# Additions to x on the gate tiles' ring, memsets on GpSimd, a shorter compressed softmax, an early Exp table and another bank for the first latent values

## The chip, the core and the metric

One core of a Trainium2 chip runs the whole kernel: TensorE (PE), VectorE (DVE), ScalarE (ACT), GpSimd (POOL) and the DMA queue of SyncE (SP). The metric is the device time in microseconds; the kernel before took 1947.82, the median of three runs (1947.81 to 1949.94).

## What is computed

Two layers of a transformer on 512 positions of width 1024, in float32. Each layer is half a SwiGLU, a mixer, half a SwiGLU, each on a normed x; the first layer's mixer is "even" (compressed, selected and sliding attention with gates, beside dilated attention), the second's is MLA (latent) attention. Cut to what matters:

```python
for l in range(DEPTH):
    x = x + 0.5 * _swiglu(_rms_norm(x, ffn1_norm[l]), ...)
    h = _rms_norm(x, mix_norm[l])
    x = x + (_even_mixer(h, ...) if l % 2 == 0 else _mla_mixer(h, ...))
    x = x + 0.5 * _swiglu(_rms_norm(x, ffn2_norm[l]), ...)
return _rms_norm(x, final_norm)
```

The compressed attention's part that the change touches: keys and values are compressed to 31 blocks of 32 positions (16 apart), and query t sees a block only if the block has ended, so the first 31 queries see none and get zero:

```python
s = jnp.where(mask, scores, -MASK_BIG)
p = jnp.where(mask, jnp.exp(s - max(s)), 0.0)
p_c = p / where(sum(p) > 0, sum(p), 1.0)
out = gate0 * (p_c @ vc) + gate1 * o_selected + gate2 * o_window
```

## The kernel before

x lies transposed, as eight tiles x[0] to x[7] of 128 features by 512 positions. Every product is made of three float32r products (high by high, low by high, high by low: `mm3`, L208 to L210), so each operand is split: `split` makes xh on ScalarE (L217) and xl on VectorE (L218), `fetch` makes wh (L160) and wl (L161) of a weight of 512 KB that SP loads two chunks ahead (L154).

Six stages follow each other: f0, e, f1, f2, m, f3 (`run`). A norm is applied late: the stage's products start from the split x, and the factor comes in when a bank of PSUM is evacuated. `norm` therefore splits x[0] to x[7] and beside it squares them on ScalarE (L229), the first into the tile "of", the others into tiles of the ring "t" (four buffers, `tmp`), adds them on GpSimd (L231, six additions; the eighth square stays by itself), sums over the partitions on TensorE (`rstd`, L241), scales on VectorE (L246), raises to the power -1/2 on GpSimd (L251, tile rcol), and spreads the factor over the partitions with four transposes (`spread`, L260) and a copy on ScalarE (L261, tile rrow).

A SwiGLU (`ffn`) works in two halves of eleven blocks of hidden features. Gate products fill banks "pa", up products "pb", the gate times the norm's factor lies in a tile "fg" (two buffers, L366 or L334, Silu in L367 or L354). At the end of a half the down-projection makes the eight blocks of x one after the other, in banks "pc" and "pt" in turn: VectorE multiplies a bank by the factor into t (L387) and adds half of it to x (L388). After the second half x is final, tile by tile. After the last stage `final` takes the same squares, sums them on TensorE (L887, first the sum of seven squares, then the eighth), turns x with transposes (L894) and writes it out (L909, L912).

The even mixer (`even`) allocates its tables and tiles over memory that the SwiGLU has released, loads the tables on SP (L540 to L551), and runs a list of work written out by hand (`EVEN`, `pipe`): first "v0", values of the dilated heads (`values`, two banks "pa", evacuated with the norm's factor in L511 and L512), then "s0", projections for the compression (`stack`), keys and queries with rope (L564 to L567, of which L566 and L567 run on GpSimd), then jobs of attention with further work between them. A job (`job`) takes scores in banks "pb", their minimum (L407), Exp (L410) and a scaling on GpSimd (L415), transposes, and products with the values. "c0" and "c1" compress (`compress`: memsets of z and vc, L668 and L685), "va" makes the values and the gates (`gate`), "p0" and "p1" are the compressed softmaxes (`cmp_probs`, thin score products L710), "o0" to "o7" are the output projection, which adds to x in L531. q is made of the roped projection by L579 and L580. MLA (`mla`) has such a list too; it begins "L2 Y0 L0 F2 A2 L1 L3 W0 V0": L0 to L3 project to the latents (and square them, L229, in "t"), F2 and A2 make and apply the factor of the key-value latent (L802, L772, L773), V0 makes the first values from it in banks "pa" (L498 to L500). Its tile of transposed probabilities has a block that is set to zero (`pt_tiles`, L472), as in the even mixer.

Order: the list is the order of the program; the scheduler lays out each engine's queue from it, giving instructions that are ready in simulated time their turn by their place in the program (`schedule_with_timeline_sim=True`, L1034). Engines take their queues in order. Tiles of one name share a ring of buffers and take them in the order of the program.

Of the kernel before, what the change touches and what calls it, by code (L numbers as in the profile page):

```python
# [3 lines left out]
P = 128  # L4
# [20 lines left out]
def raw(ap):  # L25
    return ap.bitcast(F32)
# [51 lines left out]
class Core:  # L78
# [185 lines left out]
    def rms(self, tiles, eng=None):  # L264
        col = self.rstd(self.squares(tiles, eng), D)
        return col, self.spread(col, self.keep.tile([P, SEQ], F32, name="rrow", bufs=2))

    def norm(self, gi):
        xs = [self.split(self.x[k], self.g[:, gi * 8 + k:gi * 8 + k + 1], "x", 8) for k in range(KT)]
        if gi == 0:  # L270
            with self.tc.issue_after(self.last.ins):
                col, row = self.rms(self.x, self.nc.vector)
        else:
            col, row = self.rms(self.x)
        return xs, col, row
# [64 lines left out]
    def ffn(self, name, l, gi, then=None):  # L340

        nc = self.nc
        with self.tc.tile_pool(name="ff", bufs=1, reuse_waits="tile") as sb:
            self.sb = sb
            xs, _, R = self.norm(gi)
            T = None
            for half in range(2):
                ah, al = [], []
                for i in range(HF):
                    f = half * HF + i  # L350
                    a = sb.tile([P, SEQ], F32, name="fa", bufs=2)
                    if f in SEVEN:
                        g, n = self.seven(sb, ("seven", name, l, f), xs, T, R)
                        nc.scalar.activation(g, g, AF.Silu)  # L354
                        nc.vector.scalar_tensor_tensor(a, n, -1.0, g, OP.mult, OP.mult)
                    else:
                        pgu = []
                        for w, tag in (("_g", "pa"), ("_u", "pb")):
                            h, lo = self.chunk(name + w, l, f)
                            p = self.bank(tag)  # L360
                            for k in range(KT):
                                self.mm3(p, h[:, k * P:(k + 1) * P], lo[:, k * P:(k + 1) * P], *xs[k],
                                         start=k == 0, stop=k == KT - 1)
                            pgu.append(p)
                        g = sb.tile([P, SEQ], F32, name="fg", bufs=2)
                        nc.vector.tensor_tensor(g, pgu[0], R, OP.mult)  # L366
                        nc.scalar.activation(g, g, AF.Silu)  # L367
                        nc.vector.tensor_tensor(a, pgu[1], g, OP.mult)
                    h = sb.tile([P, SEQ], F32R, name="fah", bufs=HF + 1)
                    lo = sb.tile([P, SEQ], F32R, name="fal", bufs=HF + 1)  # L370
                    nc.scalar.activation(h, a, AF.Copy)
                    nc.vector.tensor_tensor(lo, a, raw(h), OP.subtract)
                    ah.append(h)
                    al.append(lo)
                    if f == 0:
                        T = self.combine(sb, gi)
                blk, cur = 0, None
                for m in range(KT):
                    p = self.bank(("pc", "pt")[m % 2])
                    for i in range(HF):  # L380
                        if blk % 8 == 0:
                            cur = self.chunk(name + "_d", l, half, blk // 8)
                        c = slice(blk % 8 * P, blk % 8 * P + P)
                        self.mm3(p, cur[0][:, c], cur[1][:, c], ah[i], al[i], start=i == 0, stop=i == HF - 1)
                        blk += 1
                    t = self.tmp()
                    nc.vector.tensor_tensor(t, p, R, OP.mult)  # L387
                    nc.vector.scalar_tensor_tensor(self.x[m], t, 0.5, self.x[m], OP.mult, OP.add)  # L388
            if then is not None:
                then(sb)  # L390
# [78 lines left out]
    def pt_tiles(self, sb):  # L469
        t = [sb.tile([P, 11, P], F32R, name=f"pt{c}") for c in "hl"]  # L470
        for x in t:
            self.nc.vector.memset(raw(x[:, 0, :]), 0.0)  # L472
        return t

    def project(self, xs, *key):
# [4 lines left out]
                     start=k == 0, stop=k == KT - 1)  # L480
        return p

    def values(self, sb, parts, xs, scale=None, more=None):


        nc = self.nc
        n, c = len(xs), parts(0)[0].shape[-1]
        v = sb.tile([P, 4, 4, P], F32R, name="v", bufs=2)
        m = SEQ // c
        for k0 in range(0, 4, m):  # L490
            bank = self.bank("pa")
            for kt in range(k0, k0 + m):
                p = bank[:, (kt - k0) * c:(kt - k0 + 1) * c]
                t = slice(kt * P, kt * P + P)
                for k in range(n):
                    wh, wl = parts(k)
                    xh, xl = xs[k]
                    nc.tensor.matmul(p, xh[:, t], wh, start=k == 0, stop=False)  # L498
                    nc.tensor.matmul(p, xl[:, t], wh, start=False, stop=False)
                    nc.tensor.matmul(p, xh[:, t], wl, start=False, stop=k == n - 1)  # L500
                if more is not None:
                    more(kt, p[:, 256:])
            src = bank[:, :m * c].rearrange("p (a b) -> p a b", a=m)[:, :, :256].rearrange("p a (b c) -> p a b c", c=64)
            h, l = v[:, k0:k0 + m, :, 0:64], v[:, k0:k0 + m, :, 64:128]
            if scale is None:
                nc.scalar.activation(h, src, AF.Copy)
                nc.vector.tensor_tensor(l, src, raw(h), OP.subtract)
                continue
            for i in range(m):
                r = scale[:, k0 + i:k0 + i + 1]  # L510
                nc.scalar.activation(h[:, i], src[:, i], AF.Copy, scale=r)  # L511
                nc.vector.scalar_tensor_tensor(l[:, i], src[:, i], r, raw(h[:, i]), OP.mult, OP.subtract)  # L512
        return v
# [20 lines left out]
    def even(self, gi):  # L534
        nc, a, kp = self.nc, self.a, self.keep
        with self.tc.tile_pool(name="ev", bufs=1, reuse_waits="tile") as sb:
            xs, rc, R = self.norm(gi)
            CR = sb.tile([P, SEQ], F32, name="CR")
            SR = sb.tile([P, SEQ], F32, name="SR")
            nc.sync.dma_start(CR, a["cos_p"])  # L540
# [117 lines left out]
            def compress(i):  # L658
# [6 lines left out]
                                         start=l0 == 0, stop=l0 == 15)  # L665
                z = sb.tile([P, 2, 32], F32, name="z", bufs=2)
                e = sb.tile([P, 2, 32], F32, name="e", bufs=2)
                nc.vector.memset(z, 0.0)  # L668
                nc.vector.tensor_copy(z[:, :, 0:31], hid[:, :62].rearrange("p (a b) -> p a b", b=31))
                nc.scalar.activation(e, z, AF.Exp, scale=-1.0)  # L670
                nc.vector.tensor_scalar(e, e, 1.0, None, OP.add)
# [7 lines left out]
                for g in range(2):  # L679
                    hr = sb.tile([P, 4, 32], F32, name="hr")  # L680
                    nc.vector.tensor_copy(hr, z[:, g:g + 1, :].to_broadcast([P, 4, 32]))
                    vg = vp[:, 64 * g:64 * g + 64]
                    nc.tensor.matmul(vg, hr, w2[:, 1, 0:64], start=True, stop=True)
                    vc = C["v", g] = sb.tile([P, 4, P], F32R, name=f"vc{g}")
                    nc.vector.memset(raw(vc), 0.0)  # L685
                    for j in range(4):
                        s = slice(32 * j, 32 * j + 32)
                        nc.scalar.activation(vc[s, j, 0:64], vg[s], AF.Copy)
                        nc.vector.tensor_tensor(vc[s, j, 64:128], vg[s], raw(vc[s, j, 0:64]), OP.subtract)

            def gate(kt, p):

                gt = C["g"][:, kt, :]
                nc.vector.tensor_scalar(gt, p, rc[:, kt:kt + 1], None, OP.mult)
                nc.scalar.activation(gt, gt, AF.Exp, scale=-1.0)
                nc.vector.tensor_scalar(gt, gt, 1.0, None, OP.add)
                nc.vector.reciprocal(gt, gt)

            def nsa_vals():
                c = [self.chunk("ev_vsw", i) for i in range(3)]  # L700
# [3 lines left out]
            def cmp_probs(g):  # L704
# [10 lines left out]
                def sp(x):  # L715
# [3 lines left out]
                nc.vector.tensor_reduce(st[:, 0], t, AX.X, OP.min)  # L719
                nc.vector.tensor_tensor(t, t, sp(st[:, 0]), OP.subtract)  # L720
                nc.scalar.activation(t, t, AF.Exp, scale=-1.0)
                nc.gpsimd.tensor_tensor(t, t, mcmp[:, 1].unsqueeze(2).to_broadcast([P, 4, 4, 32]), OP.mult)
                nc.vector.tensor_reduce(st[:, 1], t, AX.X, OP.add)
                nc.vector.tensor_scalar(st[:, 1], st[:, 1], 1.0, None, OP.max)
                nc.vector.reciprocal(st[:, 2], st[:, 1])
                nc.vector.tensor_tensor(st[:, 2].rearrange("p (a b) -> p a b", b=4),
                                        st[:, 2].rearrange("p (a b) -> p a b", b=4),
                                        C["g"][:, :, 12 * g:12 * g + 12:3], OP.mult)
                nc.gpsimd.tensor_tensor(t, t, sp(st[:, 2]), OP.mult)
                pt = self.bank("pt")  # L730
                for qt in range(4):
                    nc.tensor.transpose(pt[:, qt * P:(qt + 1) * P], t[:, qt].rearrange("p a b -> p (a b)"),
# [19 lines left out]
    def mla(self, gi):  # L752
        nc, a, kp = self.nc, self.a, self.keep
        with self.tc.tile_pool(name="ml", bufs=1, reuse_waits="tile") as sb:
            xs, rc, R = self.norm(gi)


            CQ = [sb.tile([P, SEQ], F32, name=f"CQ{i}") for i in range(2)]
# [56 lines left out]
            def vals(g):  # L815
                vk = slice(512 + g % 2 * 256, 768 + g % 2 * 256)
                kv = W["kv"]
                vs[g] = self.values(sb, lambda k: (kv[0][:, vk], kv[1][:, vk]), [cn[2]])

            def keys(hp):  # L820
                p = self.bank("pa")
# [216 lines left out]
```

## Time and profile before

| | |
|---|---|
| median of the runs | 1947.82 us |
| time of the profiled execution | 1949.46 us |
| its span, first to last instruction | 1947.7 us |
| mean granted clock of TensorE | 0.988 |
| TensorE, products | 1906.6 us busy (98%) |
| VectorE | 1276.3 us (66%) |
| ScalarE | 875.3 us (45%) |
| GpSimd | 272.8 us (14%) |
| DMA | 174.59 MB, 90 GB/s |

In a timeline each line gives the start and the duration in us, the engine, the line of the kernel, the operation, the tiles it writes and reads, the shape and how many such instructions stand together; in brackets the idle time of the engine in front of it and the instruction that ended it. PEclk is the granted clock as a share of 2.4 GHz. Weight loads (PEld) run beside the products.

### The profile page before, as it was taken

The page shows a single profiled execution, that of the slowest core. Times are in us where ns is not written, and L with a number is a line of the kernel's source. Part 1 is how long each engine was busy: PE and PEld are TensorE (multiplying, and loading weights), DVE is VectorE, ACT ScalarE, POOL GpSimd, SP SyncE. Part 2 cuts the span into 40 slices and gives each one's busy share as a digit, 9 for nine tenths or more (in the row PEclk, how much of TensorE's full clock was granted, in tenths as well). Part 3 has the DMA queues.
Part 4 walks back from the last instruction along what each step waited for, and adds up shares of the span by engine and source line. Part 5 has one row for each costly group of instructions (what it writes and reads, how often), then busy time and mean ns, then how long its engine had stood idle before and what let it go on. Part 6 is the DMA issues. An engine that isn't in the chain of part 4 may idle for free.

```text
span 1947.7 us, 26837 instructions
## 1 busy us (share of the span) xinstructions
PE 1906.6 (98%) x10418; PEld 1653.7 (85%) x10418; DVE 1276.3 (66%) x2272; ACT 875.3 (45%) x1511; POOL 272.8 (14%) x287
## 2 busy tenths in 40 slices
PE   9999999899999999999999999999899999999997
PEld 6888998778897788888888988998788878888986
DVE  8664665468888877456656664674489786646653
ACT  7432443346576654224435432442378664324421
POOL 0000000264444400000002000000256220000001
PEclk9999999899999999999999999999999999999998
DMA  4233233322111133333332332332310123333231
GB/s 172 90 109 98 87 98 108 115 81 87 55 55 34 41 100 98 98 98 97 109 98 87 98 109 87 98 119 89 122 33 23 58 83 102 104 100 96 91 107 52
DMA packets 49839, 174.59 MB, mean 90 GB/s; under 512 B 5792, under 2 KB 6048, under 8 KB 49712
## 3 DMA queue, kind: packets, MB, share of 16 engines
q1 hardware_dynamic: 48960, 171.74, 28.1%
q8 instruction: 81, 1.33, 0.3%
q10 hardware_dynamic: 720, 1.08, 0.1%
q14 instruction: 46, 0.38, 0.1%
q0 software_dynamic: 32, 0.07, 0.0%
HBM read 170.76 MB, written 2.10 MB: 89 GB/s over the span
## 4 chain that ended last, share of the span: by engine, by line
PE 71%; issue 19%; DVE 4%; ACT 3%; POOL 2%; DMA 0%; POOLq 0%; ACTq 0%; DVEq 0%
PE pa L208 8%; PE pa L209 8%; PE pa L210 8%; PE pb L209 5%; PE pb L210 5%; PE pb L208 5%; PE pt L208 5%; PE pt L209 5%; PE pt L210 5%; PE pc L210 3%; PE pc L208 3%; PE pc L209 3%; PE pc L435 2%; PE pt L424 2%; PE pb L603 1%
## 5 line engine op out<-in xcount | busy, mean ns | idle before, releaser
L161 DVE TENSOR_TENSOR wl<-w,wh 128x1024 fp32r<-128x1024 f32 x241 | 305.2, 1267 | 247.9 <-ACT wh L160 247.4
L160 ACT ACTIVATE wh<-w 128x1024 fp32r<-128x1024 f32 x241 | 254.6, 1057 | 459.9 <-PE pt L209 188.6
L208 PE MATMUL pa<-xh,wh 128*128 128x512 f32 (+1 forms) x784 | 294.4, 376 | 5.8 <-ACT wh L160 2.3
L209 PE MATMUL pa<-xl,wh 128*128 128x512 f32 (+1 forms) x784 | 292.5, 373 | 0.0
L210 PE MATMUL pa<-xh,wl 128*128 128x512 f32 (+1 forms) x784 | 292.2, 373 | 0.0
L231 POOL TENSOR_TENSOR of<-of,t 128x512 f32<-128x512 f32 x36 | 56.0, 1554 | 1375.1 <-issue 1005.6
L209 PE MATMUL pb<-xl,wh 128*128 128x512 f32 (+1 forms) x704 | 244.2, 347 | 0.2
L208 PE MATMUL pb<-xh,wh 128*128 128x512 f32 (+1 forms) x704 | 243.9, 346 | 0.1
L210 PE MATMUL pb<-xh,wl 128*128 128x512 f32 (+1 forms) x704 | 243.5, 346 | 0.0
L208 PEld LDWEIGHTS pa<-xh,wh 128*128 128x128 f32 x784 | 148.8, 190 | 33.8 <-ACT wh L160 3.7
L210 PEld LDWEIGHTS pa<-xh,wl 128*128 128x128 f32 x784 | 148.8, 190 | 26.3 <-DVE wl L161 0.8
L209 PEld LDWEIGHTS pa<-xl,wh 128*128 128x128 f32 x784 | 149.2, 190 | 24.2 <-DVE xl L218 0.2
L209 PEld LDWEIGHTS pb<-xl,wh 128*128 128x128 f32 x704 | 133.4, 189 | 18.6 <-DVE xl L218 2.6
L208 PEld LDWEIGHTS pb<-xh,wh 128*128 128x128 f32 x704 | 133.4, 189 | 16.9 <-ACT wh L160 0.5
L210 PEld LDWEIGHTS pb<-xh,wl 128*128 128x128 f32 x704 | 133.4, 189 | 16.3 <-DVE wl L161 0.4
L180 ACT ACTIVATE wh<-w 128x512 fp32r<-128x512 f32 x72 | 45.5, 632 | 210.7 <-PE pb L209 198.4
L208 PE MATMUL pc<-fah,wh 128*128 128x512 f32 x352 | 137.0, 389 | 0.0
L209 PE MATMUL pc<-fal,wh 128*128 128x512 f32 x352 | 137.0, 389 | 0.0
L210 PE MATMUL pt<-fah,wl 128*128 128x512 f32 x352 | 136.9, 389 | 0.0
L210 PE MATMUL pc<-fah,wl 128*128 128x512 f32 x352 | 136.9, 389 | 0.0
L208 PE MATMUL pt<-fah,wh 128*128 128x512 f32 x352 | 136.9, 389 | 0.0
L209 PE MATMUL pt<-fal,wh 128*128 128x512 f32 x352 | 136.9, 389 | 0.0
(255 smaller groups left out, 4115.4 us busy)
## 6 DMA issues: line engine op xcount, KB each, us to landing
w<-f_g SPq DMA_DIRECT2D x88, 512.0 KB, 3.5
w<-f_u SPq DMA_DIRECT2D x88, 512.0 KB, 3.5
w<-f_d SPq DMA_DIRECT2D x88, 512.0 KB, 3.5
w<-ev_in SPq DMA_DIRECT2D x16, 512.0 KB, 3.5
w<-ev_out SPq DMA_DIRECT2D x8, 512.0 KB, 3.3
w<-mla_out SPq DMA_DIRECT2D x8, 512.0 KB, 3.2
x<-x SPq DMA_DIRECT2D x8, 256.0 KB, 5.1
w<-ev_vb SPq DMA_DIRECT2D x4, 512.0 KB, 3.3
```

The lines of the kernel that those rows point to most:

```text
L160: nc.scalar.activation(h[:, :cols], w[:, :cols], AF.Copy)
L161: nc.vector.tensor_tensor(l[:, :cols], w[:, :cols], raw(h[:, :cols]), OP.subtract)
L180: nc.scalar.activation(h[:, c], src, AF.Copy)
L208: nc.tensor.matmul(out, wh, xh, start=start, stop=False)
L209: nc.tensor.matmul(out, wh, xl, start=False, stop=False)
L210: nc.tensor.matmul(out, wl, xh, start=False, stop=stop)
L231: eng.tensor_tensor(parts[0], parts[0], sq, OP.add)
L424: nc.tensor.transpose(ps[:, i * P:(i + 1) * P], pt[:, c:c + P], self.ident)
L435: nc.tensor.matmul(ps[:, q0:], v(kt), PT[j][:, b, :], start=start and kt == 0 and j == 0, stop=stop and kt == 3 and j == 1)
L603: nc.tensor.matmul(ps[:, :n], q[qi][:, qt * P:(qt + 1) * P], kd[ki][j][:, :n], start=j == 0, stop=j == 1)
```

## The change

Six edits. The additions to x take their product tile from the ring "fg" instead of "t". The memsets of the attention tiles, of z and of vc go from VectorE to GpSimd. In the compressed softmax the multiplication by the mask of ones (L722) is left out; instead the first of the three gates is multiplied by the mask of the first block, which is zero just for the queries that see no block (for the others Exp of the masked scores is zero anyway). The last multiplication there (L729) goes from GpSimd to VectorE. Both mixers evaluate one dummy Exp of a column right behind their norm. MLA's first values take banks "pb".

```diff
+    def warm_exp(self):
+        e = self.keep.tile([P, 4], F32, name="rcol", bufs=16)
+        self.nc.scalar.activation(e[:, 0:1], self.x[KT - 1][:, 0:1], AF.Exp, scale=0.0)
...
-                    t = self.tmp()
+                    t = sb.tile([P, SEQ], F32, name="fg", bufs=2)
                     nc.vector.tensor_tensor(t, p, R, OP.mult)
...
-            self.nc.vector.memset(raw(x[:, 0, :]), 0.0)
+            self.nc.gpsimd.memset(raw(x[:, 0, :]), 0.0)
...
-    def values(self, sb, parts, xs, scale=None, more=None):
+    def values(self, sb, parts, xs, scale=None, more=None, tag="pa"):
...
-            bank = self.bank("pa")
+            bank = self.bank(tag)
...
             xs, rc, R = self.norm(gi)
+            self.warm_exp()
...
-                nc.vector.memset(z, 0.0)
+                nc.gpsimd.memset(z, 0.0)
...
-                    nc.vector.memset(raw(vc), 0.0)
+                    nc.gpsimd.memset(raw(vc), 0.0)
...
                 nc.vector.reciprocal(gt, gt)
+                nc.vector.tensor_scalar(gt[:, 0::3], gt[:, 0::3], mcmp[:, 1, kt, 0:1], None, OP.mult)
...
                 nc.scalar.activation(t, t, AF.Exp, scale=-1.0)
-                nc.gpsimd.tensor_tensor(t, t, mcmp[:, 1].unsqueeze(2).to_broadcast([P, 4, 4, 32]), OP.mult)
...
-                nc.gpsimd.tensor_tensor(t, t, sp(st[:, 2]), OP.mult)
+                nc.vector.tensor_tensor(t, t, sp(st[:, 2]), OP.mult)
...
             xs, rc, R = self.norm(gi)
+            self.warm_exp()
...
-                vs[g] = self.values(sb, lambda k: (kv[0][:, vk], kv[1][:, vk]), [cn[2]])
+                vs[g] = self.values(sb, lambda k: (kv[0][:, vk], kv[1][:, vk]), [cn[2]], tag="pb" if g == 0 else "pa")
```

## Rows read from the trace of the kernel before

**Rows 1.** Part 1 of the page: busy time, share and instructions of each engine.

```profile
PE 1906.6 (98%) x10418; PEld 1653.7 (85%) x10418; DVE 1276.3 (66%) x2272; ACT 875.3 (45%) x1511; POOL 272.8 (14%) x287
```

**Rows 2.** Timeline of TensorE: start, us, operation, count, [idle before, releaser].

```profile
372.30 0.58 PE L499 MATMUL pa<-wh,xl 128*128 128x256 f32 x1 [2.06 <-DVE xl L218]
...
383.75 1.12 PE L260 MATMUL pt<-ident,rcol 128*128 128x128 f32 x4 [1.78 <-POOL rcol L251]
...
386.53 0.76 PE L208 MATMUL pa<-xh,wh 128*128 128x512 f32 x1 [1.66 <-DVE v L512]
...
429.59 0.50 PE L603 MATMUL pb<-kh,q 128*128 128x512 f32 x1 [2.92 <-DVE mn L407]
...
505.94 0.80 PE L208 MATMUL pa<-oh,wh 128*128 128x512 f32 x1 [3.06 <-DVE x L531]
...
593.78 3.21 PE L710 MATMUL pt<-kcmp,q 128*128 128x32 f32 x28
...
608.26 0.66 PE L732 MATMUL pt<-ident,t 128*128 128x128 f32 x4 [1.33 <-POOL t L729]
...
1401.54 0.95 PE L241 MATMUL pt<-ones,t 128*128 128x1 f32 x8
...
1412.22 0.58 PE L498 MATMUL pa<-wh,cnh 128*128 128x256 f32 x1 [4.96 <-ACT t L229]
...
1934.03 1.87 PE L887 MATMUL pt<-ones,of 128*128 128x1 f32 x8 [4.51 <-POOL of L231]
```

**Rows 3.** Stretches: length, busy PE, PEld, DVE, ACT, POOL (instructions), PEclk, DMA, GB/s.

```profile
372.00:376.00 4.00, 3.70 (x18) 3.70 (x19) 0.25 (x1) 0.36 (x1) 3.84 (x3) 0.57 0.31 113
386.00:390.00 4.00, 3.47 (x10) 2.79 (x10) 0.77 (x2) 0.23 (x1) 2.07 (x2) 0.58 0.10 38
597.00:601.00 4.00, 4.00 (x12) 3.10 (x12) 3.28 (x7) 1.06 (x1) 1.37 (x2) 0.58 0.00 0
1412.00:1420.00 8.00, 7.78 (x31) 7.37 (x32) 6.50 (x14) 3.76 (x7) 1.62 (x1) 0.50 0.00 1
```

**Rows 4.** Timeline of ScalarE (ACT): squares of the norms.

```profile
314.96 0.61 ACT L229 ACTIVATE of<-x 128x512 f32<-128x512 f32 x1
...
365.80 1.66 ACT L229 ACTIVATE t<-x 128x512 f32<-128x512 f32 x3
...
1929.26 2.19 ACT L229 ACTIVATE t<-x 128x512 f32<-128x512 f32 x4 [6.85 <-DVE x L388]
```

**Rows 5.** Timeline of GpSimd (POOL), start of the even mixer.

```profile
366.49 9.59 POOL L231 TENSOR_TENSOR of<-of,t 128x512 f32<-128x512 f32 x6 [340.04 <-ACT t L229]
```

**Rows 6.** Timeline of VectorE (DVE), start of the even mixer.

```profile
365.02 0.69 DVE L387 TENSOR_TENSOR t<-pt,rrow 128x512 f32<-128x512 f32 x1 [3.10 <-PE pt L210]
...
366.19 1.02 DVE L685 MEMSET vc<- 128x512 f32 x2
367.13 1.21 DVE L388 SCALAR_TENSOR_TENSOR x<-t,x 128x512 f32<-128x512 f32 x1
...
370.50 1.75 DVE L218 SCALAR_TENSOR_TENSOR xl<-x,g,xh 128x512 fp32r<-128x512 f32 x1
```

**Rows 7.** Groups of instructions by line: busy us, mean ns, idle before.

```profile
L415 POOL TENSOR_SCALAR p<-p,mn 128x128 f32<-128x128 f32 (+1 forms) x96 | 53.1, 558 | 73.2 <-DVE mn L411 66.4 <-PE pa L210 5.2 <-DVE z L669 0.8
```

**Rows 8.** Timeline of ScalarE: the first Exp of the even mixer.

```profile
423.81 1.28 ACT L410 ACT_TABLE_LOAD   x1
425.11 0.40 ACT L410 ACTIVATE p<-p,mn 128x128 f32<-128x128 f32 x1
```

**Rows 9.** Timelines of VectorE and GpSimd around the compressed softmaxes.

```profile
500.24 2.85 DVE L580 SCALAR_TENSOR_TENSOR q<-t,q 64x512 fp32r<-64x512 f32 x2
...
505.26 0.63 DVE L531 TENSOR_TENSOR x<-pa,x 128x512 f32<-128x512 f32 x1
...
606.72 1.48 POOL L729 TENSOR_TENSOR t<-t,st 128x512 f32<-128x512 f32 x1 [1.09 <-DVE st L726]
```

**Rows 10.** Timeline of VectorE in front of the first latent values.

```profile
1410.18 0.69 DVE L773 SCALAR_TENSOR_TENSOR cnl<-t,cnh 128x512 fp32r<-128x512 f32 x1 [0.70 <-ACT cnh L772]
```

## The prediction

> **What bounds the kernel.** The page comes first: TensorE is busy for 1906.6 of 1947.7 us [rows 1], so what can be won is its 41 us without work and what its clock withholds. The products themselves stay as they are. The timeline of TensorE, read for idle time, then gives the places [rows 2]. These touch the change: 2.06, 1.78 and 1.66 us where the even mixer begins, 2.92 us in its first scores, 3.06 and 1.33 us around the two compressed softmaxes, 4.96 us in front of the first latent values of MLA, and, last in the span, 4.51 us in front of the final norm's sums. They are eight, 22.3 us in all. The table by stretches adds the clock [rows 3]: from 372 to 376 us it is granted at 0.57 and from 386 to 390 at 0.58, mixtures of the two levels (1.2 and 2.4 GHz), and from 1412 to 1420 at 0.50, the lower level throughout. Each begins at or after one of these waits. A stretch in which TensorE is busy throughout loses its length times what is not granted: 1.7 us, 1.7 us and 4.0 us. The stretch 597 to 601 is a warning: clock 0.58, no idle time in it, and in front of it stand 28 thin score products of the second compressed softmax [rows 2]. So not every loss of clock goes with a wait.
>
> **Why the additions to x matter.** In a down-projection, L387 writes a tile of the ring "t" (four buffers), and so do the squares of the next norm (L229), all but the first, which go to "of". The trace shows what follows: the square into "of" runs at 314.96, as soon as its x is there, while those into "t" come in a bunch at 365.80, after the last L387, and at the end of the kernel four come together at 1929.26 [rows 4]. GpSimd therefore adds the squares up in six additions in a row, 9.59 us, after the projection, and its power for the norm's factor comes behind them [rows 5]. With L387 on the ring "fg" (used by gates that are long done by then), a square needs only its own x; the eight are made one after the other over the whole projection, so only the last square is left at its end, and GpSimd's last addition is a block old. The new reuse of "fg" makes L387 wait for the L388 of two blocks before: nothing. Memory that lay under "fg" is released by the last L388 instead of the last gate, so a table's DMA of the mixer may wait on SP until 368.3, with the other tables and the next weights behind it; these weights wait for a buffer until later anyway, so I cost it at nothing, and at 3 us if that cover goes.
>
> **The terms**, as gains of the profiled execution.
>
> *Start of the even mixer.* VectorE does L387 at 365.02 for 0.69 and then six memsets, of which the two largest take 1.02, before L388 at 367.13: 1.4 us in which the last x waits. L388 then takes 1.21 and the split L218 1.75, against 0.69 for L387 with GpSimd at rest [rows 6]. With the memsets and the row of additions away, the split comes 1.4 + 0.5 + 1.1 = 3.0 earlier, at 369.2 instead of 372.25, and TensorE wants it at 370.2 (372.30 less 2.06). The 2.06 go. The factor comes once the last square is summed, about 371, so the 1.78 behind the power and the 1.66 behind the evacuation that needs it go too: 5.5 us. Of the clock's two losses I take one, 1.7, since the sixteen thin sums move into the first stretch. Gain 7.2; from 1.4 (only the memsets count) to 8.9.
>
> *Memsets on GpSimd.* No row shows one there. The bounds are VectorE's time for the 512 elements (0.51) and an addition of GpSimd (9.59/6 = 1.6); nearest are its one-input instructions, 0.56 in the mean [rows 7]. Six make about 3 us. They fit in front of the power; the cover is the value products between 365 and 383, without them they cost their 3 us.
>
> *Early table.* The first Exp of the even mixer is preceded at 423.81 by a table load of 1.28 us; the Exp follows 0.02 us after it [rows 8]. Moved to right behind the last square, it lies beside the value products. Its old place is on ScalarE, while the 2.92 us wait ends on VectorE, which has queued work of its own: I take 0.7; from 0 to 2.92 with 1.7 of clock, 4.6. In MLA none of the waits shown ends on it: 0. By the Trainium skill, "ScalarE: Activation LUTs", section "What ACT_TABLE_LOAD costs", a switch costs about 2.66 us, the load and a drain of 1.38. The 0.02 us in the trace leave no room for that drain in front of the Exp. By the page the term would be about 1.5 (0.7 x 2.66/1.28) instead of 0.7; the row decides.
>
> *Compressed softmax.* L722 leaves GpSimd, L729 goes to VectorE, and a gate's multiply by the mask is added four times (8 elements a partition, each well below the 0.51 of a 512-element memset: 0 beside TensorE's projections, at most 1 without them). At the first one, L580 takes 2.85 for two instructions beside GpSimd's work, and L531, on which the 3.06 wait ends, comes behind them at 505.26 [rows 9]. At 0.69 each the two would give 1.5 back; I take 1.2, from a loss of 0.7 (the new multiply lands in front of an L531) to 4.8 with its clock. At the second, L729 takes 1.48 on GpSimd and the step in front of it waits for L722; on VectorE it takes 0.69 to 1.75. The 1.33 go: 1.3, from -0.7 to 1.3. A rule speaks against this move: by the Trainium skill, "SBUF — State Buffer", section "Who interferes with whom", a VectorE instruction with two SBUF inputs that starts second is blocked for the whole of a GpSimd instruction that reads SBUF. The 1.21 and 1.75 above agree in kind. By the rule the second gain would be nil whenever a multiply of GpSimd runs first.
>
> *MLA.* V0's operand is complete at 1410.87 (L773 of 1410.18 with 0.69), but its bank only at 1412.2, after the square of another projection [rows 10]. The bank alone is worth 1.35. The rest is the norm again: its additions end about 9 us earlier, so do the factor, the latent's own factor and its application, which then fit beside the projections. All of it is 4.96 and 4.0 of clock, 9.0. I take 7.0, since the rope of the keys follows and something of 2 us is likely to show there; from 1.35 to 9.0.
>
> *End.* With six squares summed, TensorE can take the sums when its transposes end: 4.51. The first eight sums took 1.87 behind that wait, where eight at 1401.54 took 0.95 [rows 2]; there are two such sets: up to 1.8 more. I take 6.2; from 4.5 to 6.7.
>
> Sum: 7.2 + 0.7 + 1.2 + 1.3 + 7.0 + 6.2 = 23.6 us. The profiled execution took 1949.46, 1.64 above the median of the runs, 1947.82; I take the gain from the median: **1924.2 us**. The lower ends add to 5.9, the upper ends to 35.3.
>
> **Rivals.**
> - *The ring is not what holds the squares*: GpSimd's and ScalarE's queues place them late anyway. For it: GpSimd's wait before the six names one square; against it: the "of" square, which ran 50 us earlier. Then 1.4 + 0.7 + 1.2 + 1.3 + 1.35 = 6.0 remain: 1941.9. Chance 0.10.
> - *The latent chain stays in MLA*: TensorE's queue keeps the sums of the latent's squares behind later projections, and V0 gets only its bank. For it: the eight sums of 1401.54, the latent's, stand late in that queue; against it: what kept their squares back is again "t". Then 23.6 - 7.0 + 1.35 = 18.0: 1929.8. Chance 0.18.
> - *Slower, by the order*: the queues are laid out anew from simulated times (L1034), in an attention that is woven finely; VectorE takes its queue in order, and an evacuation put behind a softmax step that is not ready stalls TensorE as at 505.94. The price is 3.06 and 1.7 of clock, 4.8 each. It decides from the sixth new one on: six give 1924.2 + 28.8 = 1953. For it: such places exist; against it: the two mixers now hold two of near this size beyond their openings, 2.92 and 3.06. Chance 0.04; three to five of them, near no change, 0.05.
>
> The forecast has 0.63. The range is 1912 to 1940: the upper ends, and the first rivals nearly whole. About 0.2%, 3.9 us, is what a measurement of this kernel can tell from no change; faster by more: 0.91, within: 0.05, slower by more: 0.04.
>
> **What would show it.** Right: squares into "t" spread over the down-projections, one addition left on GpSimd at each end; no wait of TensorE at the start of the even mixer; Exp's table load beside the value products; V0 without wait; the final sums within 2 us of the last transposes. Wrong: squares still bunched, a wait over 3 us in front of V0 or of a score, GpSimd's power behind memsets, new stretches at the low clock.

## The result and the profile after

The changed kernel takes 1922.51 us in the median of four runs (1921.53 to 1924.06), the kernel before, on the same chip, 1948.68 (1947.81 to 1949.94): a ratio of 0.9866, 95% interval 0.9849 to 0.9883. That is 26.2 us faster; 1924.2 was forecast, with a range of 1912 to 1940. The profiled execution took 1922.95 us; its span, from the first instruction to the last, is 1921.2 us. TensorE is busy for 1895.0 us of it, where it was 1906.6 [rows 1].

Line numbers of the changed kernel are 5 to 8 higher than those of before (L387 is L392, L729 is L736). TensorE's timeline, at the places of [rows 2] and at the new ones:

```profile
419.62 0.80 PE L609 MATMUL pb<-kh,q 128*128 128x512 f32 x1 [2.30 <-DVE mn L412]
...
494.41 0.66 PE L739 MATMUL pt<-ident,t 128*128 128x128 f32 x4 [1.42 <-DVE t L736]
...
595.77 0.63 PE L739 MATMUL pt<-ident,t 128*128 128x128 f32 x4 [2.10 <-DVE t L736]
...
1394.10 0.48 PE L503 MATMUL pb<-wh,cnh 128*128 128x256 f32 x2
...
1403.33 0.50 PE L208 MATMUL pb<-kh,qh 128*128 128x256 f32 x2 [1.45 <-ACT kh L836]
...
1406.24 0.58 PE L209 MATMUL pb<-kl,qh 128*128 128x256 f32 x1 [2.40 <-DVE kl L837]
...
1908.12 0.95 PE L895 MATMUL pt<-ones,of 128*128 128x1 f32 x8
...
1910.38 0.95 PE L895 MATMUL pt<-ones,t 128*128 128x1 f32 x8
```

The three waits at the start of the even mixer, the one in front of V0 and the one in front of the final sums are gone; those of the compressed softmaxes now end on L736; two new ones stand in front of MLA's first scores. Stretches (columns as in [rows 3]):

```profile
367.00:376.00 9.00, 9.00 (x79) 9.00 (x78) 1.64 (x4) 2.74 (x5) 1.02 (x1) 1.00 0.52 154
376.00:390.00 14.00, 14.00 (x75) 12.03 (x74) 7.77 (x11) 5.45 (x8) 6.56 (x5) 1.00 0.34 114
...
1394.00:1404.00 10.00, 8.27 (x52) 6.87 (x50) 9.73 (x18) 6.85 (x12) 4.19 (x4) 1.00 0.17 55
1404.00:1414.00 10.00, 7.76 (x29) 6.81 (x30) 7.28 (x19) 4.63 (x13) 2.60 (x4) 0.66 0.00 0
```

At the even mixer's start TensorE works without a gap, at its full clock. In MLA it waits 1.45 us for a copy of ScalarE (L836) and 2.40 us for VectorE (L837), which is busy for 9.73 of 10 us from 1394 on, and its clock falls behind the first of the two waits. The squares, then GpSimd, then VectorE (against [rows 4 to 6]):

```profile
352.90 0.62 ACT L229 ACTIVATE t<-x 128x512 f32<-128x512 f32 x1
...
359.69 0.61 ACT L229 ACTIVATE t<-x 128x512 f32<-128x512 f32 x1
...
367.17 0.61 ACT L229 ACTIVATE t<-x 128x512 f32<-128x512 f32 x1
367.80 1.28 ACT L271 ACT_TABLE_LOAD   x1
```

```profile
360.44 1.29 POOL L231 TENSOR_TENSOR of<-of,t 128x512 f32<-128x512 f32 x1 [5.49 <-ACT t L229]
365.11 0.21 POOL L477 MEMSET pth<- 128x128 f32 x1 [3.37 <-PE pt L210]
...
365.56 0.99 POOL L691 MEMSET vc<- 128x512 f32 x2
```

```profile
365.08 0.69 DVE L392 TENSOR_TENSOR fg<-pt,rrow 128x512 f32<-128x512 f32 x1 [2.27 <-PE pt L210]
365.81 0.69 DVE L393 SCALAR_TENSOR_TENSOR x<-fg,x 128x512 f32<-128x512 f32 x1
...
367.56 0.74 DVE L218 SCALAR_TENSOR_TENSOR xl<-x,g,xh 128x512 fp32r<-128x512 f32 x1
```

Each square follows its own x, the last addition on GpSimd is a block old, and L393 and L218 take 0.69 and 0.74 where they took 1.21 and 1.75.

The stages, each measured from the end of the last addition to x of the stage in front of it to the end of its own, before and after: first network 368.3 and 366.5 us; even mixer 309.2 and 298.4; the two networks 705.3 and 705.2; MLA 195.4 and 188.4; the last network 350.9 in both; what follows it 18.5 and 11.8. So 12.6 us come from the even mixer with its start, 7.0 from MLA, 6.7 from the end.

### The profile page after: what moved, and what is told of

It reads as the page before. It is cut to its first block, busy times and chain, and to the rows that moved or that the text cites. A ratio compares the mean times of both kernels' runs of the same rounds, so it can differ in the third digit from the quotient of the medians.

```text
span 1921.2 us, 26836 instructions
## 1 busy us (share of the span) xinstructions
PE 1895.0 (99%) x10418; PEld 1646.6 (86%) x10418; DVE 1273.3 (66%) x2270; ACT 874.5 (46%) x1513; POOL 274.5 (14%) x291
## 3 DMA queue, kind: packets, MB, share of 16 engines
q8 instruction: 81, 1.33, 0.3%
## 5 line engine op out<-in xcount | busy, mean ns | idle before, releaser
L161 DVE TENSOR_TENSOR wl<-w,wh 128x1024 fp32r<-128x1024 f32 x241 | 302.2, 1254 | 238.3 <-ACT wh L160 237.2
L180 ACT ACTIVATE wh<-w 128x512 fp32r<-128x512 f32 x72 | 45.5, 632 | 208.8 <-PE pb L209 192.7
```

The costliest lines, as they stand in the source:

```text
L161: nc.vector.tensor_tensor(l[:, :cols], w[:, :cols], raw(h[:, :cols]), OP.subtract)
L180: nc.scalar.activation(h[:, c], src, AF.Copy)
```

## The experiments

Each kernel was run beside the kernel before on one chip, and the ratio is to those runs; the stage times are of the profiled execution.

| kernel | median us | ratio to before (95%) | even mixer | MLA |
|---|---|---|---|---|
| changed | 1922.5 | 0.9866 (0.9849 to 0.9883) | 298.4 | 188.4 |
| ring_alone | 1926.3 | 0.9876 (0.9861 to 0.9890) | 302.5 | 187.4 |
| no_ring | 1944.6 | 0.9965 (0.9952 to 0.9978) | 305.3 | 195.5 |
| old_bank | 1922.0 | 0.9855 (0.9841 to 0.9870) | 297.9 | 188.2 |
| dve_memsets | 1922.1 | 0.9860 (0.9843 to 0.9876) | 299.1 | 187.9 |
| no_early_table | 1924.0 | 0.9868 (0.9854 to 0.9883) | 298.7 | 187.7 |
| old_softmax | 1924.8 | 0.9873 (0.9856 to 0.9889) | 302.1 | 188.3 |
| multiply_on_gpsimd | 1930.5 | 0.9906 (0.9891 to 0.9920) | 301.9 | 191.8 |
| softmax_first | 1928.0 | 0.9893 (0.9878 to 0.9908) | 297.9 | 192.7 |
| second_softmax_first | 1930.6 | 0.9906 (0.9892 to 0.9921) | 303.4 | 191.1 |
| rope_a | 1926.0 | 0.9877 (0.9861 to 0.9894) | 298.1 | 191.5 |
| rope_pairs | 1926.6 | 0.9884 (0.9869 to 0.9898) | 298.1 | 192.4 |
| rope_low_parts | 1924.3 | 0.9870 (0.9854 to 0.9887) | 298.6 | 190.7 |

### The ring, alone and taken away

In the kernel before:

```diff
-                    t = self.tmp()
+                    t = sb.tile([P, SEQ], F32, name="fg", bufs=2)
```

> The kernel before with the one line changed: L387 writes the ring of the gate tiles. Theory (the ring holds the squares): nearly the whole gain comes from this line. Start of the even mixer 7.5 (12.6 measured for the stage, less 1.4 of memsets on VectorE and what the softmax and the table bring), MLA 6 to 7, end 6.7: 1926 to 1932 us. Rival (GpSimd's and ScalarE's queues place the squares late anyway): the time of before, 1945 to 1950 us, with squares still in a bunch at the end of each projection. Rival (the first latent values need the other bank): the end and the even mixer gain, MLA keeps a wait of several us in front of V0: 1932 to 1936 us.

And the same line undone in the changed kernel:

> The changed kernel with its additions to x back on the ring t; all other parts stay. Theory: only memsets, softmax, table and bank remain, some 4 to 8 us below before: 1940 to 1945 us, squares in bunches again, about 5 us of wait back in front of the final sums. Rival (the ring is not the holder; the other parts made the gain): 1922 to 1927 us.

Squares in ring_alone, each a down-projection's block apart as in the changed kernel:

```profile
352.80 0.62 ACT L229 ACTIVATE t<-x 128x512 f32<-128x512 f32 x1
...
359.59 0.61 ACT L229 ACTIVATE t<-x 128x512 f32<-128x512 f32 x1
```

TensorE in ring_alone, then in no_ring, at the final sums:

```profile
1911.10 0.95 PE L887 MATMUL pt<-ones,of 128*128 128x1 f32 x8
```

```profile
1929.26 1.87 PE L895 MATMUL pt<-ones,of 128*128 128x1 f32 x8 [4.51 <-POOL of L231]
```

GpSimd in no_ring, at the even mixer's start:

```profile
367.61 9.44 POOL L231 TENSOR_TENSOR of<-of,t 128x512 f32<-128x512 f32 x6
```

One line alone makes 23.8 us (1926.3 against 1950.1), of the 26.2 of the whole change. Without it the other edits make 5.5 by the medians (1944.6), 6.8 by the ratio, and the row of additions and the 4.51 us are back. The two gains add up to more than 26.2, so part of what the other edits save is saved by the ring already. Both times fall where their theories put them: the ring is what held the squares.

### The bank

```diff
-                vs[g] = self.values(sb, lambda k: (kv[0][:, vk], kv[1][:, vk]), [cn[2]], tag="pb" if g == 0 else "pa")
+                vs[g] = self.values(sb, lambda k: (kv[0][:, vk], kv[1][:, vk]), [cn[2]])
```

> The changed kernel with the first latent values back in the ring pa. Theory: the latent's chain is done at 1393.7, 0.4 us before V0 starts, so the bank is worth one evacuation: a wait of 0.5 to 1.4 us in front of V0, with or without a stretch of the clock at its lower level (1.7 to 3.4 us): 1922.5 to 1927 us. Rival (the bank is what shortens MLA): 5 us or more are lost, 1927.5 us or more.

```profile
1394.65 0.35 PE L503 MATMUL pa<-wh,cnh 128*128 128x256 f32 x1 [0.84 <-ACT wh L160]
```

V0 starts 24.9 us into the stage instead of 24.0, behind the wait of 0.84 that was expected. The time is below the expected one all the same (1922.0): TensorE has to wait around the first scores anyway, now 1.14 and 1.79 us instead of 1.45 and 2.40, and the stage is as long as ever. The bank is worth 1 us at V0 and nothing at the end.

### The memsets and the early table

In dve_memsets `nc.gpsimd.memset` goes back to `nc.vector.memset` in three places; in no_early_table both calls of `warm_exp` are taken out.

> The changed kernel with its memsets back on VectorE. Theory: 1.5 us of memsets come in front of the last split of the even mixer, which then ends at about 369.8 instead of 368.3, still before TensorE wants it (370.2 in the trace of before): 0 to 0.5 us, 1922 to 1923.5 us. Rival (the memsets hold the last split up, as the lower bound of the prediction's first term has it): a wait of 0.5 to 1.5 us at the even mixer's start, with 1.7 us of clock where it falls: 1923.5 to 1926 us.

> The changed kernel without the two early Exp instructions. Theory: a load of 1.28 us returns in front of the even mixer's first Exp; of it 0.6 to 0.7 shows, since the wait behind it ends on VectorE's queue (2.92 us before, 2.30 after the change): 1922.5 to 1924 us. Rival (the load lies beside other work): 0, the wait stays at 2.30 us, 1922 us. Rival by the Trainium skill's page ScalarE: Activation LUTs, section What ACT_TABLE_LOAD costs: its figure of 2.66 us for the switch would make the wait 1.5 us longer or more, 1924 us and above.

VectorE in dve_memsets:

```profile
368.50 0.69 DVE L393 SCALAR_TENSOR_TENSOR x<-fg,x 128x512 f32<-128x512 f32 x1
...
370.81 1.02 DVE L691 MEMSET vc<- 128x512 f32 x2
371.75 0.63 DVE L218 SCALAR_TENSOR_TENSOR xl<-x,g,xh 128x512 fp32r<-128x512 f32 x1
```

The memsets lie behind the last addition to x and hold the last split up by 1.5 us, and TensorE does not wait: 0.

ScalarE, then TensorE, in no_early_table:

```profile
414.24 1.28 ACT L415 ACT_TABLE_LOAD   x1
415.54 0.40 ACT L415 ACTIVATE p<-p,mn 128x128 f32<-128x128 f32 x1
```

```profile
420.01 0.50 PE L608 MATMUL pb<-kh,q 128*128 128x512 f32 x1 [2.92 <-DVE mn L412]
```

Without the early table the load stands in front of the first Exp again, and the wait in the first scores is 2.92 instead of 2.30 us: 0.6. In MLA, where it stands at 1406.83, the stage is no longer for it (187.7 against 188.4). The medians differ by 1.5 and the intervals overlap nearly whole; 1924.0 lies at the edge between the theory's time and the last rival's, so the 0.6 rests on the trace alone. By an estimate from the Trainium skill's figure (page "ScalarE: Activation LUTs", section "What ACT_TABLE_LOAD costs") it would have been about 1.5; the trace, with 0.62 and with the Exp 0.02 us behind the load, does not agree.

### The compressed softmax

old_softmax undoes the whole part, multiply_on_gpsimd only L736:

```diff
-                nc.vector.tensor_tensor(t, t, sp(st[:, 2]), OP.mult)
+                nc.gpsimd.tensor_tensor(t, t, sp(st[:, 2]), OP.mult)
```

> The changed kernel with the compressed softmax as it was: the mask multiply and the last multiply on GpSimd, no gate multiply. Theory (the softmax part as a whole is worth 2 to 4 us of the even mixer: the stage takes 298.4 us after the change and 302.5 with the ring alone): the 3.06 us in front of the output projection and the 1.33 at the second softmax return, the stage takes 300.5 to 302.5 us. MLA keeps its 188 us: 1924.5 to 1926.5 us; if its order shifts to the other one (191 to 192 us) 3.5 more. Rival (the two waits on L736 that the change left, 1.42 and 2.10, are as long as those that it took away): the stage takes 298 to 300 us, 1922 to 1924 us.

> The changed kernel with the last multiply of the two compressed softmaxes (L736) back on GpSimd; the removed mask multiply stays removed. Theory (on VectorE it stands behind the two L586, 1.40 to 1.86 us, so its move gained nothing at the second softmax): on GpSimd it takes about 1.5 us and starts 1.4 to 1.9 earlier: the wait of 2.10 at the second becomes 1.3 to 2.1, the first's 1.42 stays within 0.7: 1921 to 1923 us. Rival (the move to VectorE is what removed the 3.06 us in front of the output projection): this wait returns, with 1.7 of clock: 1924 to 1927 us.

TensorE in old_softmax, at the first softmax and at the second:

```profile
497.22 0.63 PE L208 MATMUL pa<-oh,wh 128*128 128x512 f32 x1 [3.06 <-DVE x L536]
...
594.83 0.50 PE L208 MATMUL pa<-oh,wh 128*128 128x512 f32 x1 [1.60 <-DVE x L536]
...
599.19 0.66 PE L739 MATMUL pt<-ident,t 128*128 128x128 f32 x4 [1.30 <-POOL t L736]
```

TensorE in multiply_on_gpsimd, at the first, and the GpSimd instruction that it waits for:

```profile
495.90 0.66 PE L739 MATMUL pt<-ident,t 128*128 128x128 f32 x4 [2.77 <-POOL t L736]
```

```profile
493.93 1.91 POOL L736 TENSOR_TENSOR t<-t,st 128x512 f32<-128x512 f32 x1 [2.83 <-DVE st L733]
```

The part is worth 3.6 us of the mixer (302.1 against 298.4): about 1.4 at the first softmax (3.06 against 1.42 and 0.21), 1.4 at the second (1.60, 1.30, 0.66 and two small waits against 2.10 and three small ones), the rest with the clock. Both times expected of multiply_on_gpsimd failed: it takes 1930.5, its theory said at most 1923 and its rival at most 1927. The two L586 stand ahead of the reduction in front of L736 in either kernel (from 490.33 in the changed one, from 490.49 here), so at the first softmax GpSimd has no head start: L736 starts at 493.93, on VectorE it started at 493.66. There it takes 1.91 us on GpSimd, beside VectorE's two-input L161 of 493.71 and 1.23; at the second softmax it takes 1.05. On VectorE it takes 0.69 at both. Of the 8 us, 3.5 are the mixer's and 3.4 MLA's, where TensorE's order came out anew.

Two kernels move a projection of the queries out of the softmax's way in the list `EVEN` (of its line only the part that differs is shown):

```diff
-    ... "q10 p0", "", "q2", ...
+    ... "p0", "", "q2 q10", ...
```

> The changed kernel with one entry of the even mixer's list moved: q10 (whose rope puts two L586 between the first compressed softmax's steps) two places later, behind p0. Theory (VectorE's queue in front of L736 makes the waits of 1.42 and 2.10 us): without L586 there the first wait falls under 0.7 us; the second, where L586 has also gone from in front of L736, under 1.2, with the clock's 1.7 us behind it kept or gone: 1919 to 1921.5 us. Rival (the softmax's own chain is as long as its cover): the waits stay, 1921.5 to 1924 us. Rival (the later query is late, or MLA's order shifts by 3.5 us): 1924 to 1927 us.

```diff
-    ... "o2 p1 q11 o3", "", ...
+    ... "o2 p1 o3", "q11", ...
```

> The changed kernel with q11 moved one place later, behind the second compressed softmax, instead of between it and o3. Theory: the two L586 leave the place in front of the second L736, its wait of 2.10 us falls to 0.7 or less, with the clock's 1.7 us behind it kept or gone: 1919 to 1921.5 us. Rival (the projections that q11 brought were the cover of this softmax): the wait grows by up to the 5 us of one projection, 1924 to 1927 us.

TensorE in softmax_first, then in second_softmax_first:

```profile
492.06 0.66 PE L739 MATMUL pt<-ident,t 128*128 128x128 f32 x4 [0.45 <-DVE t L736]
...
651.66 0.73 PE L208 MATMUL pa<-oh,wh 128*128 128x512 f32 x2 [2.06 <-ACT oh L622]
```

```profile
597.98 0.49 PE L440 MATMUL pc<-pth,v 128*128 128x512 f32 x1 [0.72 <-ACT pth L432]
599.09 0.44 PE L429 MATMUL pt<-ident,p 128*128 128x128 f32 x2 [0.62 <-DVE cl L744]
```

In softmax_first the waits on L736 did go (0.45 and none), as the theory has it, but the mixer is only 0.6 us shorter: 1.24 us (on VectorE's L433) stand at the second softmax and 2.06 us in front of the last output projections, perhaps because less work is left to cover them; no run shows that. The networks behind came out 1.3 us longer and MLA 4.3. In second_softmax_first the 2.10 became waits of 0.72 and 0.62, the same 2.06 appeared at the end, and the stage is 5.0 longer. Both kernels are slower than any time that was expected of them (at most 1927), and not through the wait that the rivals name.

### MLA's first scores

In the list `MLA`, for rope_a (the opening entry):

```diff
-"L2 Y0 L0 F2 A2 L1 L3 W0 V0 F1 R1 Q0 Q1 R0 K0"
+"L2 Y0 L0 F2 A2 L3 L1 W0 V0 R0 F1 R1 Q0 Q1 K0"
```

> The changed kernel with MLA's opening list reordered: the projection of the rope part (L3) goes ahead of L1, and the first rotary copies ahead of the second factor. Theory: the 1.45 and 2.40 us in front of MLA's first scores, and the clock's loss of 3.4 us behind them, come from the rope of the keys, which is made last; a projection earlier it is done in time: 4 to 7 us less, 1915.5 to 1918.5 us. Rival (VectorE's queue in front of the keys' low part ends these waits wherever the rope stands): 1921 to 1924 us. Rival (L1 later makes the queries late): a wait in front of the same scores on the factor of the queries, 1922 to 1927 us.

For rope_pairs `R1` moves to the head of the next fill, and its copies are placed behind the first keys':

```diff
-                    nc.scalar.activation(kt_[i][0][r], t[r], AF.Copy)
-                    nc.vector.tensor_tensor(kt_[i][1][r], t[r], raw(kt_[i][0][r]), OP.subtract)
+                    with self.tc.issue_after(c["high"]) if n else contextlib.nullcontext():
+                        nc.scalar.activation(kt_[i][0][r], t[r], AF.Copy)
+                    with self.tc.issue_after(c["low"]) if n else contextlib.nullcontext():
+                        nc.vector.tensor_tensor(kt_[i][1][r], t[r], raw(kt_[i][0][r]), OP.subtract)
```

> The changed kernel with MLA's second pair of rotary copies (for heads 2 and 3) issued behind the first keys' copies on ScalarE and VectorE, instead of ahead of the first pair; nothing else is moved. Theory (the queue in front of the first scores, not the length of the rope's own chain, makes the 1.45 and 2.40 us of wait): two copies of 0.65 leave ScalarE's queue and two of 0.71 VectorE's; the 1.45 us go, the 2.40 shrink to 1.0 to 1.8; with the clock's loss of 3.4 kept 1919 to 1921 us, with it gone 1916 to 1919 us. Rival (the rope's chain through GpSimd is the limit): both waits stay, 1921.5 to 1924 us. Rival (the second query is now late by the two copies): a new wait of about 1.3 us in front of the second head's scores, 1921 to 1923 us.

rope_low_parts moves `R1` too, but keeps only the second of the two `issue_after`.

> As rope_pairs, but only the low parts of the second pair (VectorE) go behind the first keys' low part; ScalarE keeps its four high parts ahead of the keys' high part. TensorE's order of the attention behind it is then nearly that of the changed kernel, while in rope_pairs it is nearly that of the kernel before. From V0 to its last addition to x the stage took 162.4 to 164.4 us in the three runs with the first order that were looked at (ring_alone, old_bank, the changed kernel) and 166.1 to 168.5 with the second (before, rope_a, rope_pairs). Theory (the order that comes out behind the start decides, and rope_pairs lost by it what its start had won): the wait of 1.45 us stays, the 2.40 shrink by 1.0 to 2.0, and the stage from V0 takes 161 to 163.5 us: 1919 to 1922 us. Rival (the second pair is needed early, wherever the order puts the rest): the stage from V0 takes 166 us or more, 1924 to 1927 us.

TensorE in rope_a, rope_pairs and rope_low_parts, in this order:

```profile
1397.58 0.50 PE L209 MATMUL pa<-cnl,wh 128*128 128x512 f32 x1 [1.32 <-DVE cnl L781]
1399.84 1.50 PE L241 MATMUL pt<-ones,t 128*128 128x1 f32 x9 [1.53 <-ACT t L229]
```

```profile
1403.52 0.39 PE L209 MATMUL pb<-kl,qh 128*128 128x256 f32 x1 [1.14 <-DVE kl L839]
1406.25 0.69 PE L208 MATMUL pb<-kh,qh 128*128 128x384 f32 x1 [1.86 <-DVE mn L412]
```

```profile
1403.50 0.51 PE L208 MATMUL pb<-kh,qh 128*128 128x256 f32 x2 [1.45 <-ACT kh L838]
1404.22 0.39 PE L209 MATMUL pb<-kl,qh 128*128 128x256 f32 x1 [0.21 <-DVE kl L839]
1407.22 0.58 PE L503 MATMUL pa<-wh,cnh 128*128 128x256 f32 x1 [2.27 <-DVE v L512]
```

Each time the wait aimed at shrank or went, and waits on other instructions, most of them in VectorE's queue, took its place: the latent's low part, the first minimum, the evacuation of V0's values. In rope_a it is the late L1 that is waited for, as its last rival has it, and that rival's time was met. VectorE is busy for 9.6 to 9.8 of 10 us at the start in all three, as in the changed kernel, and the waits there sum to 3.3, 3.0 and 3.9 us, where they were 3.9: the order chose who waits and took off little. rope_pairs is slower than any time that was expected of it; its stage is 4.0 us longer, and all of that lies behind V0.

The last theory, that TensorE's order behind the start decides, missed its time (161 to 163.5): from V0 on rope_low_parts takes 166.7 us (1394.28 to 1560.99), which is the rival's, 2.3 more than the changed kernel. That does not refute it yet. The trace gives 1.4 of them to the clock, which falls a second time, behind two waits of 0.67 and 0.66 us, and 0.5 to more waiting:

```profile
1443.00:1447.00 4.00, 4.00 (x17) 3.53 (x17) 3.91 (x13) 1.02 (x4) 2.10 (x4) 0.57 0.01 2
```

What is left, the time in which TensorE works from V0 on less what the lower clock takes from it, is 156.2 us (the changed kernel's is 155.8). It is 155.8 to 156.2 in all kernels with a stage of 187 to 188 us and 157.2 to 158.5 in all others, so here rope_low_parts goes with the fast ones. Why the same products take 1 to 3 us more in one order than in another stays open; no kernel here moves that alone.

No kernel beats the changed one by more than the intervals; old_bank and dve_memsets are its equals.

## Why the prediction was right

The mechanism is the one that was forecast: the squares were held by the ring "t", and with them the additions, the factor and the sums at both ends. Three stretches more bear on what the clock gave back (columns as in [rows 3]; the first two before the change, the third after it):

```profile
382.00:386.00 4.00, 1.12 (x4) 0.72 (x4) 1.57 (x5) 1.93 (x5) 1.45 (x2) 0.57 0.80 226
1934.00:1938.00 4.00, 3.63 (x17) 3.57 (x18) 0.16 (x1) 0.00 (x0) 0.00 (x0) 0.50 0.00 0
```

```profile
1908.00:1912.00 4.00, 4.00 (x40) 4.00 (x39) 2.06 (x5) 0.63 (x1) 0.33 (x1) 1.00 0.00 0
```

The sizes of the terms came out as follows.

- **Start of the even mixer**, 7.2 forecast: the score product behind the 0.73 us of wait (at 422.46 before) stands at 413.12, and at 413.00 in ring_alone: 9.3 to 9.5, just over the upper end of 8.9. Mis-sized was the clock, "of the clock's two losses I take one": both came back (1.00 from 367 to 390). And the second was larger than the row of 386 to 390 shows, since it began at 382.6 already: TensorE worked for 4.0 us in it, so it cost 2.0, and 5.5 of waits, 1.7 and 2.0 make 9.2. The ring also took the memsets out from between L387 and L388; in ring_alone they are still VectorE's, and its x is done at 366.4 all the same. The later release of the memory under "fg" cost nothing, as forecast: no wait of TensorE follows it.
- **Memsets**: 0, right. The six take 1.4 us on GpSimd, not about 3; 0.99 for the two large ones is VectorE's own time [rows 6].
- **Early table**: 0.6, 0.7 forecast; by the trace alone.
- **Compressed softmax**: 2.5 forecast; against its own undoing 2.8 by the waits, 3.6 with the clock. In the second term "the 1.33 go" was wrong as it stands: a wait of 2.10 is there, on L736 behind L586; what went is its sum with those around it. The Trainium skill's rule ("SBUF — State Buffer", section "Who interferes with whom") did not make the gain nil: L736 on VectorE takes its 0.69 unblocked. On GpSimd it is the second of two such instructions itself, and takes 1.91 behind L161 where it takes 1.05 at the other softmax: there the trace agrees with the rule.
- **MLA**: 7.0 forecast, 7.05 measured; that the two agree so closely is luck, for the sum is put together otherwise. V0 starts 5.4 us earlier in its stage (24.0 instead of 29.3). "Something of 2 us" at the rope of the keys is 1.45 and 2.40, 3.85 of waits, and the clock loses 3.4 behind them (0.66 over 10 us), nearly the 4.0 of before, which the term had given back whole. For all that the stage from V0 on is 1.7 shorter (164.4 instead of 166.1). By the windows from V0 to the stage's end the waits elsewhere are 1.75 us instead of some 3.4, and TensorE's work, less the clock's loss, is 2.5 shorter (155.8 instead of 158.3). The prediction did not foresee either, and their cause is not shown. The lower end, 1.35 for the bank alone, did not hold without the ring: in no_ring V0 starts 2.0 earlier and the stage is as long as before (195.5 and 195.4).
- **End**: 6.7, 6.2 forecast: 4.51 and 0.35 of wait, and 1.8 from sums of 0.95 instead of 1.87 and 1.84. The sums are shorter by the clock: 0.50 at them before, behind the wait, and 1.00 now.
- **Rivals**: the first is refuted by ring_alone and no_ring (it left 6.0 us to the other edits, and without the ring they make 5.5); the second by the trace (V0 without wait) and by old_bank; of the third, two new waits came (1.45 and 2.40) and two in old places (1.42 where 3.06 was, 2.10 where 1.33 was), far from the six of 4.8 that it needs.

## What to carry to other kernels

When a row of small operations waits until a loop has ended, look at which ring of buffers it shares with the loop before looking at its engine: here one line's choice of buffer, alone, gave 23.8 us, and the whole change 26.2. Where a timeline shows an engine's queue full in front of a wait, expect a new order of that queue to move the wait to another consumer: three orders here left 3.0 to 3.9 of 3.9 us. That less work in the queue would shorten it is likely, but no run here tries it. And where the instruction order is laid out by a planner, a small move can change a stage far behind it by 3 to 4 us, as MLA shows in the three kernels that moved a step of the even mixer's softmax (2.7 to 4.3), so an edit's worth is read stage by stage, not from the total.

## What the runs showed of the hardware

A multiplication of 128x4 elements on VectorE took 1.22 us in front of the keys' low part (1404.36 to 1405.58) and ended when GpSimd's two-input L850 ended (1403.88 and 1.69):

```profile
1404.36 1.22 DVE L253 TENSOR_TENSOR rcol<-rcol 128x4 f32<-128x4 f32 x1
```

```profile
1403.88 1.69 POOL L850 TENSOR_TENSOR ql<-t,qh 128x512 fp32r<-128x512 f32 x1 [0.72 <-ACT qh L849]
```

In rope_low_parts, with GpSimd idle at 1403.38, it took 0.16. By the Trainium skill, "SBUF — State Buffer", section "Who interferes with whom", a VectorE instruction with two inputs in SBUF is blocked by a GpSimd instruction that reads SBUF and came first; the trace agrees, and here a tiny instruction paid the whole rest of GpSimd's.

The same wait does not always cost the same clock. Behind the wait of 2.10 us at the second softmax the clock falls in the changed kernel; in dve_memsets, behind a wait of 2.09 us in the same place, it does not (the changed kernel, then dve_memsets):

```profile
596.00:600.00 4.00, 4.00 (x20) 3.28 (x19) 4.00 (x10) 2.67 (x6) 0.00 (x0) 0.57 0.37 110
```

```profile
599.75 0.63 PE L739 MATMUL pt<-ident,t 128*128 128x128 f32 x4 [2.09 <-DVE t L736]
```

```profile
600.00:604.00 4.00, 3.53 (x25) 2.74 (x24) 4.00 (x11) 2.59 (x7) 0.00 (x0) 1.00 0.37 104
```

So a difference of up to 1.7 us between two stage times here can be the clock's alone. It can also be lower in places that no edit touches: in dve_memsets' profiled execution from 0 to 24 us,

```profile
0.00:24.00 24.00, 18.77 (x56) 11.85 (x57) 16.14 (x24) 16.46 (x24) 0.95 (x5) 0.86 0.66 235
```

where the changed kernel's shows 1.00. TensorE also waits three times there, 2.0 us in all, for split weights that the changed kernel has in time, and the first network ends 2.7 us later (369.2 against 366.5).
